# Gate projections of a decoder layer: seven-product pairs fed by one transfer each, fewer of them, their sums spread out

## The chip, the cores and the metric

The kernel runs on one core of a Trainium2 chip. The metric is the device time of one execution in microseconds. The times shown are medians of several executions of the same program.

## The reference

One layer of a hybrid decoder for 16 learned and 256 given positions of width 2048, in float32. Only the part that the change touches is told closely.

```python
h = h + 0.5 * swiglu(rms_norm(h), ...)                  # first feed-forward half step
z = rms_norm(h) @ w_in                                  # one projection, 11 parts
q, k, v, qi, ki, wi, xc, gate_b, gate_c, ga, gc = split(z)
y_attn = sparse_attention(q, k, v, qi, ki, wi) @ w_attn_branch
y_conv = (gate_b * causal_conv3(gate_c * xc)) @ w_conv_branch
merged = sigmoid(ga) * y_attn + sigmoid(gc) * y_conv    # the gate stage computes this line
h = h + merged @ w_out
h = h + 0.5 * swiglu(rms_norm(h), ...)                  # second feed-forward half step
```

`ga` and `gc` are each 256 positions by 2048 columns, with 2048 inputs: two matrix products of 256 x 2048 by 2048 x 2048.

## The kernel before

**Splitting of weights.** Every float32 weight block arrives by DMA in a tile `raw` (SP issues the transfers), is rounded by ScalarE into `whi` (line 227), and VectorE writes the rest `raw - whi` into `wlo` (line 228). Activations are split in the same way. Each product is three matmuls: high by high, high by low, low by high (`mac3`, lines 613 to 615, for products in which the tokens are the stationary operand and 512 weight columns move).

**The stream.** The class `Stream` holds the list of all weight transfers (`loads`) and of the parts of them that are split in one go (`subs`, at most 1024 columns). `next` hands out one weight block after another. When a part is used up it runs what is due, then splits the part that lies three ahead, then runs the `later` list. The split tiles have four buffers, so the split of a part can begin only when TensorE has finished the part four before it. Each engine works through its instructions in the order in which they are written, so whatever is written ahead of a `wlo` on VectorE delays it.

**The ring.** `raw` has 12 slots of 512 columns (256 KB each). A transfer is issued as soon as the slots it wants have been split (`load`); it then waits for the splits of their former owner.

**Gate stage.** The 2048 output columns are done in four blocks `c` of 512 (`gates(c)`), for `ga` and `gc` together. The 2048 inputs form eight pairs of 256. One pair is a product of a 2 by 2 arrangement: two token tiles and two input tiles on one side, two input tiles and two outputs (`ga`, `gc`) on the other. Kind `C` does it with the plain eight products of four weight blocks, accumulated in the PSUM banks `q2`, `q3`, `q4`, `q8`. The other kind does it with seven products, as Strassen and Winograd do: the weight side needs sums of the blocks, the token side needs sums of the token tiles, which are made once per pair (`sums_of_tokens`, tiles `made`) and used in all four column blocks, and seven banks collect the products. At the end of a block `recombine` (lines 696 to 701) turns banks `q1`, `q5`, `q6`, `q7` into the four results, one step after another, and `after_end` (line 1193) adds what the plain pairs collected.

After the eight pairs come the branch products of the block: `y_attn` and `y_conv` by 512 columns, 32 products into the banks `pbr`. `merge` (lines 1218, 1220) multiplies gates and branches at the start of the next block. Ahead of the last half pair the merged block before is turned by TensorE (`pt`, line 666) and split into `ms` (lines 438, 439).

**Kind Q, the seven-product pair of before.** It takes two loads of four blocks `[a21, a22, a11, a12]` (the order in memory), and a second time the last three of them in two more loads: 7 blocks of 256 KB. `sum_ahead` (line 212) makes the four sums in place in the first four blocks, one directly after the other, when the part before them is about to be split. The plain blocks for the other products are the second copy. Parts of the pair: 2, 2, 2 and 1 blocks.

Block 0 takes the kinds `CCCQQQCC`, the later blocks `CQQCQQCC`; `SEVEN` lists the pairs with sums of tokens, (3, 5, 7, 1), made while block 0 runs.

Around the stage nothing is touched: the convolution stage before it, the output projection `po` (line 417) after it and the second feed-forward, which has seven-product pairs of another kind (`P`, whose sums are made long before and stored).

Of the kernel before, what the change touches and what calls it, by code (L numbers as in the profile page):

```python
# [9 lines left out]
F32 = mybir.dt.float32  # L10
# [5 lines left out]
P = 128  # L16
D = 2048
# [34 lines left out]
WIDE = 512  # L52
NG = FF // WIDE
PAIRS = KD // 2
# [3 lines left out]
PLAN = [step for gs in PARTS for step in [("up", g) for g in gs] + [("down", gs)]]  # L58


SEVEN = (3, 5, 7, 1)
SUMS = ((1, 1, 0), (0, 0, 2), (2, 2, 1), (3, 3, 2))
SEVEN2 = (3, 5, 7, 1, 6)
LATE = (8, 4)
# [5 lines left out]


def pairs_gate(c):
    return list(zip("CCCQQQCC", [0, 2, 4, 3, 5, 7, 6, 1]) if c == 0 else zip("CQQCQQCC", [0, 3, 5, 2, 7, 1, 4, 6]))


def pairs_down(gs, half):
# [21 lines left out]
class Stream:  # L98
# [7 lines left out]
    def __init__(self, nc, raw, split_pool):  # L106
        self.nc = nc
        self.ring = [(raw, i) for i in range(2 * SLOTS)]
        self.owner, self.pos = {}, 0
        self.split_pools, self.ahead, self.n_tiles = [split_pool], AHEAD, 0  # L110
        self.loads, self.subs = [], []
        self.raw, self.ready, self.summed = {}, {}, set()
        self.n_loaded = self.n_split = self.at = 0
        self.blocks, self.waiting, self.steps = [], [], []
        self.first = []
        self.ahead_of, self.prep = [], []
# [13 lines left out]
    def add_pair(self, kind, four, ahead):  # L130

        if kind == "C":
            self.add(four.pop(0), 4, WIDE, False)
            return
        if kind == "P":
            src, made = ahead.pop(0)
            self.ahead_of.append((src, made))
            self.add(made, 4, WIDE, False)
            self.add(src[:, WIDE:], 3, WIDE, False)
            return  # L140
        src = ahead.pop(0)
        g = len(self.subs)
        self.add(src, 4, WIDE, False)
        self.add(src[:, WIDE:], 3, WIDE, False)
        self.subs[g] = (self.subs[g][0], "sums") + self.subs[g][2:]

    def widen(self, raw, split_pool):

# [54 lines left out]

    def sum_ahead(self):

        for g, kind, _, _, _ in self.subs[self.n_split : self.n_split + 2]:
            if kind == "sums" and g not in self.summed:
                self.load(g + 2)
                self.summed.add(g)
                x = [self.raw[g + j // 2][:, j % 2 * WIDE : (j % 2 + 1) * WIDE] for j in range(4)]  # L210
                for out, a, b in SUMS:
                    self.nc.vector.tensor_add(x[out], x[a], x[b])

    def split(self, upto):
        nc = self.nc
        while self.n_split < min(upto, len(self.subs)):
            self.sum_ahead()
            g, kind, c, kk, width = self.subs[self.n_split]
            self.load(len(self.loads))
            n = kk * width  # L220
            raw = self.raw[g][:, c : c + n]
            pool = self.split_pools[self.n_tiles % len(self.split_pools)]
            self.n_tiles += 1
            hi = pool.tile([P, SUB], F32R, name="whi")
            lo = pool.tile([P, SUB], F32R, name="wlo")
            to = [x[:, :n] for x in (hi, lo)]
            nc.scalar.activation(to[0], raw, AF.Copy)  # L227
            nc.vector.tensor_sub(to[1], raw, to[0].bitcast(F32))  # L228
            self.ready[self.n_split] = [
                (hi[:, i * width : (i + 1) * width], lo[:, i * width : (i + 1) * width]) for i in range(kk)  # L230
            ]
            self.n_split += 1
            self.load(len(self.loads))
# [48 lines left out]
def tile_decoder_layer(  # L282
# [13 lines left out]
    wq: bass.AP,  # L296
    wcv: bass.AP,
    wg: bass.AP,
    wgq: bass.AP,
    wb: bass.AP,  # L300
    wo: bass.AP,
    w2: bass.AP,
# [14 lines left out]
    st = Stream(nc, raw_pool.tile([P, SLOTS * SUB], F32, name="raw"), split_pool)  # L317
# [18 lines left out]
    chunks(wq, 0, 8, 512)  # L336
    units2 = len(st.subs)
    chunks(wcv, 0, 3 * KC)
    wg_c, wg_q, w2_c, w2_p = ([w[i] for i in range(w.shape[0])] for w in (wg, wgq, w2, w2p))
    scratch = ctx.enter_context(tc.tile_pool(name="scratch", bufs=1, space=bass.MemoryType.DRAM))  # L340
    w2_p = [(w, scratch.tile([P, RAW], F32, name=f"sums{i}")) for i, w in enumerate(w2_p)]
    for c in range(D // WIDE):
        for kind, _ in pairs_gate(c):
            st.add_pair(kind, wg_c, wg_q)
        for i in range(KC // 2):
            st.add(wb[c * KC // 2 + i], 4, WIDE, False)
    for a, b in ((0, 12), (12, KD)):
# [8 lines left out]
    h = hp.tile([P, KD, T], F32, name="h")  # L356
# [5 lines left out]
    small = const.tile([P, SMALL], F32, name="small")  # L362
    ident = const.tile([P, P], F32, name="ident")
# [314 lines left out]
    def group(todo, hook, after_seven, after_end, spread=(1, 2, 3, 4)):  # L678

        kinds = [k for k, _, _ in todo]  # L680
        nc_ = kinds.count("C")
        ns = len(kinds) - nc_
        last = max(n for n, k in enumerate(kinds) if k != "C")
        q = {}

        def of(tag):
            if tag not in q:
                q[tag] = [bank(tag, tag), 0, {"q2": ns + 2 * nc_, "q3": ns + 2 * nc_, "q4": ns + 2 * nc_, "q8": 2 * nc_}.get(tag, ns)]
            return q[tag]

        buf = {}

        def recombine():
            a, v, x, e = (small_tile(n) for n in "avxe")
            buf.update(q2=a, q3=v, q4=x, q8=e)
            nc.scalar.activation(a, q["q1"][0], AF.Copy)
            steps = [
                lambda: nc.vector.tensor_sub(v, q["q6"][0], a),
                lambda: nc.vector.tensor_add(x, q["q7"][0], v),
                lambda: nc.vector.tensor_sub(v, q["q5"][0], v),  # L700
                lambda: nc.vector.scalar_tensor_tensor(e, q["q5"][0], -1.0, x, op0=ALU.mult, op1=ALU.add),
            ]
            soon = spread and not spread[0]
            if soon:
                steps[0]()
            for i, fn in list(enumerate(steps))[bool(soon) :]:
                st.later(fn, spread[i] if spread else 1)
            if after_seven:
                for i, tag in enumerate(buf):
                    st.later(lambda tag=tag: after_seven(tag, buf[tag]), 5 + i // 2 if spread else 2)  # L710

        for n, (kind, four, ts) in enumerate(todo):
            b11, b12, b21, b22 = four()
            if kind != "C":
                t1, t3, t2, t4 = (both(ts()[:, :, f * P : (f + 1) * P]) for f in range(4))
                todo7 = [("q7", t3), ("q5", t1), ("q6", t2), ("q3", b22), ("q4", t4), ("q1", b11), ("q2", b21)]
                for tag, t in todo7:
                    mac3(of(tag), t, st.next())
                if n == last:
                    st.early(recombine)  # L720
            else:
                plain_half(b11, b12, b21, b22, of("q2"), of("q3"))
                if n == len(todo) - 1:
                    st.early(lambda: after_end(q, buf, ("q2", "q3")))
                hook(n)
                plain_half(b11, b12, b21, b22, of("q4"), of("q8"), not spread and n == len(todo) - 1)
        st.early(lambda: after_end(q, buf, ("q4", "q8")))

    with ExitStack() as mix:
# [434 lines left out]
        gp = mix.enter_context(tc.tile_pool(name="gates", bufs=1, reuse_waits="tile"))  # L1164
        room.append(gp)

        act1 = act[:, :, :, LATER + META : LATER + T]
        made1 = {i: gp.tile([P, 2, 4 * P], F32R, name=f"made{i}") for i in SEVEN}
        for at, (i, to) in zip((0, 3, 7, 16), made1.items()):
            sums_of_tokens(i, gains[1], to, at)  # L1170

        ms, merged = {}, []
# [233 lines left out]


_INS = [
    "h", "small", "rope", "cbias", "ident", "wgu1", "wd1", "wk", "wkw", "wv", "wqi", "wq", "wcv", "wg", "wgq", "wb",
    "wo", "w2", "w2p",  # L1410
]

# [27 lines left out]
def _quads(kind, w0, w1, i, j0, j1):  # L1440

    rows = [w[2 * i * P : (2 * i + 2) * P, j * WIDE : (j + 1) * WIDE].reshape(2, P, WIDE) for w, j in ((w0, j0), (w1, j1))]
    (a11, a12), (a21, a22) = rows
    return np.concatenate(
        {"C": [a12, a11, a22, a21], "P": [a21, a22, a11, a12], "Q": [a21, a22, a11, a12]}[kind], 1
    )


def _by_kind(chunks, kinds):
    return [np.stack([x for k, x in chunks if k == kind]) for kind in kinds]  # L1450


def _gates(ga, gc):
    return _by_kind([(k, _quads(k, ga, gc, i, c, c)) for c in range(D // WIDE) for k, i in pairs_gate(c)], "CQ")


def _second(wg, wu, wd):
# [34 lines left out]
def _layout(x, meta_tokens, ffn1_norm_g, ffn1_w_gate, ffn1_w_up, ffn1_w_down, mix_norm_g, w_in, q_norm_g,  # L1492
# [21 lines left out]
    w = w_in[0]  # L1514
# [4 lines left out]
    a["wkw"] = _tiles(np.concatenate([ki, wi], 1), NKW)[0]  # L1519
    a["wqi"], a["wq"] = _chunks(_tiles(qi, 512)), _chunks(_tiles(q, 512))  # L1520
    a["wcv"] = np.stack([_tiles(xc, P), _tiles(gc_, P), _tiles(gb, P)], 1).reshape(3 * KC, P, KD * P)
    a["wg"], a["wgq"] = _gates(ga, gcv)
    wb = np.stack([w_attn_branch[0], w_conv_branch[0]]).reshape(2, KC, P, D // WIDE, WIDE).transpose(3, 1, 2, 0, 4)
    a["wb"] = np.ascontiguousarray(
        wb.reshape(D // WIDE, KC // 2, 2, P, 2 * WIDE).transpose(0, 1, 3, 2, 4).reshape(-1, P, RAW)
# [23 lines left out]
```

## Time and profile before

| what | value |
|---|---|
| median of three executions | 2140.4 us (2139.38 to 2141.89) |
| the profiled execution | 2142.07 us, its span 2140.3 us |
| granted TensorE clock, mean | 0.997 |
| busy TensorE, weight loads, VectorE, ScalarE | 2113.4, 1904.6, 1676.7, 1132.9 us |
| DMA | 617.24 MB, 288 GB/s on average |
| gate stage | 1087.1 to 1362.9 us |

PE is TensorE's matmuls, PEld its weight loads (they overlap), DVE VectorE, ACT ScalarE, POOL GpSimd, SP the engine that issues the weight transfers. A line of a timeline gives start, duration, engine, source line, operation, `out<-in` with tile names, shape and count; in brackets stands the idle time ahead of it and what ended it. A matmul row lasts longer than its share of the engine, since matmuls are pipelined: the distance from one start to the next tells the rate. A line of the list of waits gives the waiting engine with its instruction, what it waited for, the total in us, how often, and the longest.

### The profile page before, as it was taken

Reading aid. Unit: us, or ns where it says so; the run is one execution under the profiler, and the core shown is the slowest. Engines: PE = TensorE matmul, PEld = TensorE weight load, DVE = VectorE, ACT = ScalarE, POOL = GpSimd, SP = SyncE. Lnnn points to the kernel's source line nnn. Section 1 sums busy time; section 2 is a strip of 40 time slices with the busy share of each in tenths; the row PEclk is TensorE's granted clock in tenths of the full one; section 3 lists DMA queues with packets and bytes.
Section 4 is the critical chain, followed back from the end, with each engine's and each line's share of the span. In section 5 each row is a group of like instructions: output and inputs, shape, how many; then the busy total and the mean of one; then the engine's idle time right before and its main releaser. Section 6 shows DMA issues by size and latency. Waiting matters only on the chain.

```text
span 2140.3 us, 33445 instructions
## 1 busy us (share of the span) xinstructions
PE 2113.4 (99%) x12961; PEld 1904.6 (89%) x12961; DVE 1676.7 (78%) x2214; ACT 1132.9 (53%) x1469; POOL 114.8 (5%) x190
## 2 busy tenths in 40 slices
PE   8999999999999999999999999999999999999999
PEld 8999999999999999889987877888888888888887
DVE  7777766677777767887787878587888888988887
ACT  5444433344444445465455555476766667666664
POOL 2000000000000110000000000010000000000000
PEclk9999999999999999999999999999999999999999
DMA  7899999999999967845676677467787888788875
GB/s 282 307 350 360 361 350 371 355 360 364 352 369 354 358 232 256 348 172 198 239 235 223 228 252 229 163 225 245 274 314 282 287 319 303 292 274 301 310 268 177
DMA packets 128895, 617.24 MB, mean 288 GB/s; under 512 B 14336, under 2 KB 14464, under 8 KB 86624
## 3 DMA queue, kind: packets, MB, share of 16 engines
q1 hardware_dynamic: 107712, 463.52, 60.6%
q0 software_dynamic: 20880, 151.42, 18.8%
q8 instruction: 101, 1.65, 0.3%
q14 instruction: 58, 0.48, 0.1%
q10 hardware_dynamic: 144, 0.17, 0.0%
HBM read 537.46 MB, written 77.59 MB: 287 GB/s over the span
## 4 chain that ended last, share of the span: by engine, by line
PE 92%; DVE 4%; DMA 2%; ACT 1%; issue 1%; POOL 0%; SPq 0%; ACTq 0%; DVEq 0%
PE q L614 12%; PE q L615 12%; PE q L613 12%; PE pd L402 4%; PE pd L403 4%; PE pd L404 4%; PE pg L404 4%; PE pu L404 4%; PE pg L402 4%; PE pu L402 4%; PE pg L403 4%; PE pu L403 4%; PE po L417 3%; DVE wlo L228 2%; PE po L419 1%; PE pbr L613 1%
## 5 line engine op out<-in xcount | busy, mean ns | idle before, releaser
L227 ACT ACTIVATE whi<-raw 128x1024 fp32r<-128x1024 f32 (+2 forms) x927 | 926.9, 1011 | 903.1 <-PE q L615 264.3
L228 DVE TENSOR_TENSOR wlo<-raw,whi 128x1024 fp32r<-128x1024 f32 (+2 forms) x927 | 1060.5, 1164 | 396.7 <-ACT whi L227 385.5
L614 PE MATMUL q<-wlo,act 128*128 128x512 f32 x713 | 279.5, 392 | 11.3 <-DVE wlo L228 11.3
L613 PE MATMUL q<-whi,act 128*128 128x512 f32 x713 | 280.0, 393 | 0.0
L615 PE MATMUL q<-whi,act 128*128 128x512 f32 x713 | 279.2, 392 | 0.0
L167 DVE TENSOR_TENSOR prep<-prep 128x512 f32<-128x512 f32 x288 | 196.9, 684 | 15.7 <-DMA prep<-in_w2p_dram 15.5
L402 PE MATMUL pd<-mid,whi 128*128 128x272 f32 x704 | 201.7, 286 | 0.0
L403 PE MATMUL pd<-mid,whi 128*128 128x272 f32 x704 | 201.7, 286 | 0.0
L404 PE MATMUL pd<-mid,wlo 128*128 128x272 f32 x704 | 201.7, 286 | 0.0
L402 PE MATMUL pg<-act,whi 128*128 128x272 f32 x672 | 192.7, 287 | 0.0
L404 PE MATMUL pg<-act,wlo 128*128 128x272 f32 x672 | 192.5, 287 | 0.0
L403 PE MATMUL pg<-act,whi 128*128 128x272 f32 x672 | 192.5, 287 | 0.0
L402 PE MATMUL pu<-act,whi 128*128 128x272 f32 x672 | 192.5, 286 | 0.0
L403 PE MATMUL pu<-act,whi 128*128 128x272 f32 x672 | 192.5, 286 | 0.0
L404 PE MATMUL pu<-act,wlo 128*128 128x272 f32 x672 | 192.5, 286 | 0.0
L614 PEld LDWEIGHTS q<-wlo,act 128*128 128x128 f32 x713 | 134.6, 189 | 40.5 <-DVE wlo L228 13.0
L615 PEld LDWEIGHTS q<-whi,act 128*128 128x128 f32 x713 | 134.7, 189 | 28.2
L613 PEld LDWEIGHTS q<-whi,act 128*128 128x128 f32 x713 | 134.6, 189 | 27.5
L402 PEld LDWEIGHTS pd<-mid,whi 128*128 128x128 f32 x704 | 132.6, 188 | 0.0
L403 PEld LDWEIGHTS pd<-mid,whi 128*128 128x128 f32 x704 | 132.6, 188 | 0.0
L404 PEld LDWEIGHTS pd<-mid,wlo 128*128 128x128 f32 x704 | 132.6, 188 | 0.0
L403 PEld LDWEIGHTS pg<-act,whi 128*128 128x128 f32 x672 | 126.6, 188 | 0.0
(273 smaller groups left out, 3802.5 us busy)
## 6 DMA issues: line engine op xcount, KB each, us to landing
raw<-in_wgu_dram SPq DMA_DIRECT2D x87, 1024.0 KB, 6.5
prep<-in_w2p_dram POOLq DMA_DIRECT2D x72, 1024.0 KB, 9.1
sums<-prep POOLq DMA_DIRECT2D x72, 1024.0 KB, 5.7
raw<-sums SPq DMA_DIRECT2D x144, 512.0 KB, 5.7
raw<-in_w_dram SPq DMA_DIRECT2D x120, 512.0 KB, 6.4
raw<-in_wd_dram SPq DMA_DIRECT2D x44, 1024.0 KB, 8.1
raw<-in_w2p_dram SPq DMA_DIRECT2D x72, 512.0 KB, 5.7
raw<-in_wcv_dram SPq DMA_DIRECT2D x24, 1024.0 KB, 4.8
```

The lines of the kernel that those rows point to most:

```text
L167: nc.vector.tensor_add(x[out], x[a], x[b])
L227: nc.scalar.activation(to[0], raw, AF.Copy)
L228: nc.vector.tensor_sub(to[1], raw, to[0].bitcast(F32))
L402: nc.tensor.matmul(ps, whi, xhi, start=first, stop=False)
L403: nc.tensor.matmul(ps, whi, xlo, start=False, stop=False)
L404: nc.tensor.matmul(ps, wlo, xhi, start=False, stop=last)
L417: nc.tensor.matmul(ps.rearrange("p (a t) -> p a t", a=2), whi, x(i), start=i == 0, stop=False)
L419: nc.tensor.matmul(ps[:, :SEQ], wlo, x(i)[:, 0, :], start=False, stop=i == total - 1)
L613: nc.tensor.matmul(ps, xhi, whi, start=n == 0, stop=False)
L614: nc.tensor.matmul(ps, xhi, wlo, start=False, stop=False)
L615: nc.tensor.matmul(ps, xlo, whi, start=False, stop=n == total - 1)
```

## The change

A new kind `S` takes the place of `Q` in the gate stage.

- An S pair is loaded once, four blocks `[a21, a11, a22, a12]` in two loads.
- Three of its sums go into a new tile `extra` of 3 x 512 columns, one is made in place. Parts of the pair: `extra` 0 and 1; the two blocks of the first load, the first of them now a sum; the two blocks of the second load; `extra` 2.
- The four sums are made in three goes (two, one, one), each just ahead of the split of the part before the one that needs them. A part whose sums cannot be made yet, since `extra` does not exist before the stage, is not split.
- The seven products come in another order, to follow the parts.
- Block 0 takes `CCCSCSCC` with its pairs in their natural order, the later blocks `CSSCSCCC`. So there are 2 + 3 x 3 = 11 seven-product pairs instead of 3 + 3 x 4 = 15. Pair 1 becomes plain everywhere, its sums of tokens are not made, and those of pair 7 are made later.

```diff
-SEVEN = (3, 5, 7, 1)
+SEVEN = (3, 5, 7)
...
-    return list(zip("CCCQQQCC", [0, 2, 4, 3, 5, 7, 6, 1]) if c == 0 else zip("CQQCQQCC", [0, 3, 5, 2, 7, 1, 4, 6]))
+    return list(zip("CCCSCSCC", range(PAIRS)) if c == 0 else zip("CSSCSCCC", [0, 3, 5, 1, 7, 2, 4, 6]))
...
-        src = ahead.pop(0)
-        g = len(self.subs)
-        self.add(src, 4, WIDE, False)
-        self.add(src[:, WIDE:], 3, WIDE, False)
-        self.subs[g] = (self.subs[g][0], "sums") + self.subs[g][2:]
+        g, n = len(self.loads), len(self.subs)
+        self.add(ahead.pop(0), 4, WIDE, False)
+        self.subs[n:] = [(g, "sums", 0, 2, WIDE), (g, "raw", 0, 2, WIDE), (g + 1, "raw", 0, 2, WIDE), (g + 1, "sums", 2 * WIDE, 1, WIDE)]
+
+        def add(*abc):
+
+            def block(i):
+                x = self.extra if i < 3 else self.raw[g + (i - 3) // 2]
+                i = i if i < 3 else (i - 3) % 2
+                return x[:, i * WIDE : (i + 1) * WIDE]
+
+            def fn():
+                self.load(g + 2)
+                for to, a, b in abc:
+                    self.nc.vector.tensor_add(block(to), block(a), block(b))
+
+            return fn
+
+        self.sums.update({n: add((0, 3, 4), (1, 3, 5)), n + 1: add((3, 1, 4)), n + 2: add((2, 3, 6))})
...
-        for g, kind, _, _, _ in self.subs[self.n_split : self.n_split + 2]:
-            if kind == "sums" and g not in self.summed:
-                self.load(g + 2)
-                self.summed.add(g)
-                x = [self.raw[g + j // 2][:, j % 2 * WIDE : (j % 2 + 1) * WIDE] for j in range(4)]
-                for out, a, b in SUMS:
-                    self.nc.vector.tensor_add(x[out], x[a], x[b])
+        for n in (self.n_split, self.n_split + 1):
+            if n in self.sums and self.extra is not None:
+                self.sums.pop(n)()
...
             self.sum_ahead()
+            if self.n_split in self.sums:
+                return
...
-            raw = self.raw[g][:, c : c + n]
+            raw = (self.extra if kind == "sums" else self.raw[g])[:, c : c + n]
...
                 todo7 = [("q7", t3), ("q5", t1), ("q6", t2), ("q3", b22), ("q4", t4), ("q1", b11), ("q2", b21)]
+                if kind == "S":
+                    todo7 = [todo7[i] for i in (0, 1, 2, 5, 4, 6, 3)]
...
+        st.extra = gp.tile([P, 3 * WIDE], F32, name="extra")
         act1 = act[:, :, :, LATER + META : LATER + T]
         made1 = {i: gp.tile([P, 2, 4 * P], F32R, name=f"made{i}") for i in SEVEN}
-        for at, (i, to) in zip((0, 3, 7, 16), made1.items()):
+        for at, (i, to) in zip((0, 3, 16), made1.items()):
```

More of the change, by code (lines that the diff above doesn't have):

```diff
@@ L111, in __init__ @@
         self.loads, self.subs = [], []
-        self.raw, self.ready, self.summed = {}, {}, set()
+        self.raw, self.ready, self.sums, self.extra = {}, {}, {}, None
         self.n_loaded = self.n_split = self.at = 0
@@ L298, in tile_decoder_layer @@
     wg: bass.AP,
-    wgq: bass.AP,
+    wgs: bass.AP,
     wb: bass.AP,
@@ L338, in tile_decoder_layer @@
     chunks(wcv, 0, 3 * KC)
-    wg_c, wg_q, w2_c, w2_p = ([w[i] for i in range(w.shape[0])] for w in (wg, wgq, w2, w2p))
+    wg_c, wg_s, w2_c, w2_p = ([w[i] for i in range(w.shape[0])] for w in (wg, wgs, w2, w2p))
     scratch = ctx.enter_context(tc.tile_pool(name="scratch", bufs=1, space=bass.MemoryType.DRAM))
@@ L343, in tile_decoder_layer @@
         for kind, _ in pairs_gate(c):
-            st.add_pair(kind, wg_c, wg_q)
+            st.add_pair(kind, wg_c, wg_s)
         for i in range(KC // 2):
@@ L1408 @@
 _INS = [
-    "h", "small", "rope", "cbias", "ident", "wgu1", "wd1", "wk", "wkw", "wv", "wqi", "wq", "wcv", "wg", "wgq", "wb",
+    "h", "small", "rope", "cbias", "ident", "wgu1", "wd1", "wk", "wkw", "wv", "wqi", "wq", "wcv", "wg", "wgs", "wb",
     "wo", "w2", "w2p",
@@ L1444, in _quads @@
     return np.concatenate(
-        {"C": [a12, a11, a22, a21], "P": [a21, a22, a11, a12], "Q": [a21, a22, a11, a12]}[kind], 1
+        {"C": [a12, a11, a22, a21], "P": [a21, a22, a11, a12], "S": [a21, a11, a22, a12]}[kind], 1
     )
@@ L1453, in _gates @@
 def _gates(ga, gc):
-    return _by_kind([(k, _quads(k, ga, gc, i, c, c)) for c in range(D // WIDE) for k, i in pairs_gate(c)], "CQ")
+    return _by_kind([(k, _quads(k, ga, gc, i, c, c)) for c in range(D // WIDE) for k, i in pairs_gate(c)], "CS")
 def _second(wg, wu, wd):
@@ L1521, in _layout @@
     a["wcv"] = np.stack([_tiles(xc, P), _tiles(gc_, P), _tiles(gb, P)], 1).reshape(3 * KC, P, KD * P)
-    a["wg"], a["wgq"] = _gates(ga, gcv)
+    a["wg"], a["wgs"] = _gates(ga, gcv)
     wb = np.stack([w_attn_branch[0], w_conv_branch[0]]).reshape(2, KC, P, D // WIDE, WIDE).transpose(3, 1, 2, 0, 4)
```

## The prediction

> **What bounds the kernel now.** I read the page first (busy times, then the chain of work that ended last), then the waits cut to the stretch that the diff touches, then a table of that stretch by stage, then the timelines of TensorE and VectorE around each stall.
>
> ```profile
> span 2140.3 us, 33445 instructions
> ...
> PE 2113.4 (99%) x12961; PEld 1904.6 (89%) x12961; DVE 1676.7 (78%) x2214; ACT 1132.9 (53%) x1469; POOL 114.8 (5%) x190
> ```
>
> TensorE is never idle for long: 26.9 us of 2140.3. So time can only be won where it waits or runs slowly, and every matmul added is paid in full. The waits between 1080 and 1365 us, which hold the gate stage:
>
> ```profile
> PE q L614 <- DVE wlo L228: 11.7, 6, 3.4
> ...
> DVE raw L212 <- DMA raw<-in_wgq_dram: 9.4, 6, 2.6
> ...
> PE pbr L613 <- DVE ms L439: 1.4, 2, 1.2
> ```
>
> The first row is the same (11.7 us) in the list for the whole kernel: all of it lies here. Next the gate stage, cut at the first matmul of each block's pairs and of its branch products (columns: window, its length, then busy time with instruction count of PE, PEld, DVE, ACT, POOL, then the granted clock, DMA share, GB/s):
>
> ```profile
> 1087.10:1134.00 46.90, 44.16 (x185) 35.22 (x184) 41.86 (x59) 27.83 (x37) 0.73 (x1) 0.96 0.73 245
> 1134.00:1155.76 21.76, 21.76 (x97) 18.02 (x96) 14.69 (x16) 12.12 (x13) 0.00 (x0) 1.00 0.58 176
> 1155.76:1202.65 46.89, 43.62 (x189) 35.63 (x188) 41.30 (x49) 24.88 (x27) 0.00 (x0) 0.96 0.78 261
> 1202.65:1224.41 21.76, 21.76 (x97) 18.02 (x96) 14.54 (x17) 10.95 (x12) 0.00 (x0) 1.00 0.56 163
> 1224.41:1271.44 47.03, 43.65 (x190) 35.62 (x188) 41.29 (x49) 24.77 (x27) 0.00 (x0) 0.96 0.76 257
> 1271.44:1293.20 21.76, 21.76 (x98) 18.02 (x96) 14.55 (x17) 10.95 (x12) 0.00 (x0) 1.00 0.55 170
> 1293.20:1339.19 45.99, 43.65 (x189) 35.63 (x188) 39.92 (x48) 24.08 (x26) 0.00 (x0) 0.96 0.78 251
> 1339.19:1362.92 23.73, 22.28 (x98) 17.86 (x96) 12.76 (x16) 11.44 (x15) 0.00 (x0) 1.00 0.56 195
> ```
>
> A branch stage has 16 weight blocks x 2 token tiles x 3 matmuls = 96, and runs without a gap: 21.76 / 96 = 0.227 us a matmul, 0.68 us a product of three. That is the ruler. Block 0 has 3 Q and 5 C pairs, 3x7 + 5x8 = 61 products; the later ones 4x7 + 4x8 = 60, and 0.79 us of transposes, which stand in the middle of the last pair:
>
> ```profile
> 1199.03 1.03 PE L666 MATMUL pt<-ident,vm 128*128 128x128 f32 x8
> 1199.82 0.47 PE L613 MATMUL q<-whi,act 128*128 128x512 f32 x1
> ```
>
> So the four pair stages should last 41.5, 41.6, 41.6, 41.6 us, and lose 5.4, 5.3, 5.4 and 4.4; the last branch stage loses 23.73 - 21.76 = 2.0. Together **22.5 us**, twice the 11.7 of the wait list. The other half is in the matmuls behind a stall:
>
> ```profile
> 1115.71 0.50 PE L614 MATMUL q<-wlo,act 128*128 128x512 f32 x1 [2.32 <-DVE wlo L228]
> ...
> 1177.11 0.50 PE L614 MATMUL q<-wlo,act 128*128 128x512 f32 x1 [3.27 <-DVE wlo L228]
> ...
> 1178.69 0.63 PE L614 MATMUL q<-wlo,act 128*128 128x512 f32 x1
> 1179.11 0.63 PE L615 MATMUL q<-whi,act 128*128 128x512 f32 x1
> ...
> 1245.88 0.50 PE L614 MATMUL q<-wlo,act 128*128 128x512 f32 x1 [3.38 <-DVE wlo L228]
> ...
> 1313.62 0.50 PE L614 MATMUL q<-wlo,act 128*128 128x512 f32 x1 [2.34 <-DVE wlo L228]
> ```
>
> After the wait the matmuls follow 0.43 us apart, not 0.23, for about eight of them; the window's granted clock is 0.96 against 1.00 in the branch stages. Of block 1's 5.3 us, 3.4 are the gap and 1.9 the slow clock. The other three long waits have their slow stretch behind them too.
>
> Why the wait? VectorE around block 1, then the link that the chain of work shows between its last `wlo` and the late sum:
>
> ```profile
> 1155.53 0.69 DVE L1218 TENSOR_TENSOR va<-pbr,va 128x512 f32<-128x512 f32 x1
> ...
> 1159.12 2.35 DVE L228 TENSOR_TENSOR wlo<-raw,whi 128x1024 fp32r<-128x1024 f32 x2
> 1161.39 2.86 DVE L212 TENSOR_TENSOR raw<-raw 128x512 f32<-128x512 f32 x4
> 1164.17 5.83 DVE L228 TENSOR_TENSOR wlo<-raw,whi 128x512 fp32r<-128x512 f32 x6
> 1172.45 0.69 DVE L212 TENSOR_TENSOR raw<-raw 128x512 f32<-128x512 f32 x1 [2.45 <-DMA raw<-in_wgq_dram]
> ```
> ```profile
> 1167.15 6.54 DMA raw<-in_wgq_dram
> ```
>
> The third Q pair's sums stand in VectorE's queue ahead of a `wlo` that TensorE needs sooner, and wait there for a load that could start only at 1167.15, when a `wlo` of the second pair freed its slots. A Q takes 7 of the ring's 12 slots, so the ring reaches 1.7 pairs ahead. Block 0 has no such DMA wait: there three Q in a row with the sums of tokens simply overfill VectorE:
>
> ```profile
> 1103.81 2.87 DVE L212 TENSOR_TENSOR raw<-raw 128x512 f32<-128x512 f32 x4
> ```
>
> **The change, part by part.**
>
> *Matmuls.* Block 0 goes from 3 seven-product pairs to 2, the others from 4 to 3: one product more each, 4 x 3 x 0.227 = **+2.7 us**, on the path with nothing to cover it.
>
> *Loads.* A Q brings 1.75 MB in four transfers, an S 1 MB in two, like a C. 15 Q + 17 C make 43.25 MB, 11 S + 21 C 32 MB; 30 fewer issues on SP. Every pair now takes 4 slots, so the ring reaches 3 pairs. When is the load for block 1's third S due? Count from 1155.76 as 0. It takes the slots of the first S's second load, free when that pair's last `wlo` is done, about 8.0 (below). The landing times of these loads:
>
> ```profile
> DMA to landing us min/median/max: 2.8/4.4/6.9
> ```
>
> So it is there at 12.5, or 15 at worst; its first sum comes up on VectorE at 14.4 and TensorE does not need what stands behind it until 17.9. The DMA wait goes; what is late next is VectorE itself.
>
> *VectorE per pair.* The number of sums stays four per pair. The rows price them: four in a burst 1161.39 to 1164.17, 0.70 each, where each waits for the one ahead of it; independent ones of this size start 0.60 apart (1155.53 to 1159.12, six). A full `wlo` is 2.27 / 2 = 1.13, a half one 0.60. An S so costs 2.4 to 2.8 + 3 x 1.13 + 0.6 = 6.4 to 6.8 us against 4.76 us of its matmuls; a C 2.3 against 5.44. I take 0.60 for a sum, since the new order puts a `wlo` between dependent ones, and keep 0.70 for the bound.
>
> *Order.* The sums now come as two, one and one, each ahead of another `wlo`. Block 1 is C S S C S C C C. By the rows above, VectorE merges the branches from -0.23 until 3.36, with the first S's first `wlo` already behind it. Then: third sum of S1 3.96, `wlo` 5.10, 6.23, two sums of S2 7.43, S1's half `wlo` 8.03, sum 8.63, `wlo` of S2's first part 9.77 (TensorE wants it at 10.21 + 0.23 = 10.44), sum 10.37, `wlo` of the second 11.50 plus 0.09 to be seen (wanted 11.80), third 12.64 (13.16), half 13.24 (14.5), C 14.38 (15.2), two sums of S4 15.58, `wlo` 16.7 (17.9). The tightest point has 0.2 us. With sums at 0.70, five of them ahead of it, it is 0.3 late. ACT is not in the way: `whi` of that part can start when the sum is done at 8.63 and takes 1.06. I book 0.3 us a block, from 0 to 0.8.
>
> *Block 0.* C C C S C S C C: the S stand apart, and S plus C is 6.4 + 2.3 = 8.7 on VectorE against 10.2 on TensorE. The sums of tokens for pair 1 fall away, those for pair 7 move to the late place. I book 0.2.
>
> *Last branch stage.* The wait there is for `ms`, which stands behind two steps of `recombine` (700, 701):
>
> ```profile
> 1336.25 0.68 DVE L700 TENSOR_TENSOR vv<-q,vv 128x512 f32<-128x512 f32 x1
> ...
> 1339.78 0.42 DVE L439 TENSOR_TENSOR ms<-pt,ms 128x256 fp32r<-128x256 f32 x1
> ```
>
> In the later blocks the last seven-product pair is now the fifth, not the sixth, so these two steps (1.2 us) come one pair earlier. Of 2.0 us, 0.5 stay (0 to 2.0).
>
> *Tile `extra`.* The next pair's two sums overwrite it three parts after their last reader; no wait. It and one `made` tile fewer shift later tiles of the pool; their former users are a stage old. Nothing, with the first C pair (8 x 0.68 = 5.4 us) as cover: the first sum comes up only behind it; without that cover the first sum would wait for the last user of the old pool.
>
> *A rule beside the rows.* The slow stretch follows waits of 2.3 to 3.4 us, four times of four, and is absent in the branch stages. The Trainium skill (TensorE: Matmul & The Clock Gate, Part 1) has the clock halve after at least one idle window of about 3.4 us, free-running. Taken by the letter, these waits would be too short, the slow stretch would have another cause and stay; see the third rival.
>
> **Sum.** -22.5 (all lost time) + 2.7 (matmuls) + 0.3 x 3 + 0.2 + 0.5 (what stays lost) = **-18.2 us**, -0.85%. The profiled execution took 2142.07 us (span 2140.3, 1.8 around it), 1.7 above the median of 2140.4; against the median that makes **2122.2**. With nothing left lost: 2140.4 - 19.8 = 2120.6.
>
> **Rivals.**
>
> 1. *VectorE stays late at two S in a row, and the clock drops behind it.* A stall of 0.5 us with the slow stretch of 1.9 in three blocks: 7.2 instead of 0.9, so -11.9: 2128.5. For it: the margin of 0.2 us after 11.7 us of unbroken VectorE work. Against: the sums got cheaper, and the slow stretch followed no wait under 2.3 us (the 1.2 us wait at `pbr` had none).
> 2. *The DMA wait stays in the three later blocks.* Only block 0 is cured: -5.4 + 2.7: 2137.7, within 0.2%. It decides if the third S's load lands after about 16, 8 us after its slots are free; the slowest landing so far is 6.9.
> 3. *The slow stretches have another cause.* About 2.1 + 3 x 1.9 = 7.8 us stay lost: 2130. Against it stands their place, right behind each wait and nowhere else in the stage. The rule above gives this result.
> 4. *Slower: VectorE and ACT alternate instead of overlapping within an S*, since each part's `whi` now waits for a sum that stands behind the part before. Then an S takes (1.4 + 1.06 + 1.22) + (0.7 + 1.06 + 1.22) + 2.3 + 2.0 = 11 us against 4.76; two in a row run 12.5 behind, a lead of some 5 covers part, with the slow clock 9 us a block instead of the 5.0 on average now: 3 x 4 + 2.7 - 5.4 = +9: 2150. It decides from about 2.5 us more per S. Against: each sum stands ahead of a `wlo` that belongs to an earlier part, so ACT works under it.
>
> **How the numbers follow.** Main case 0.75, rivals 0.10, 0.05, 0.04 and 0.04, the rest unnamed and on both sides. Two executions differ by some 0.1% here (2139.38 to 2141.89), so 0.2%, 4.3 us, is what can be told from no change. Faster: main, first and third rival, 0.90; same: the second, 0.05; slower: the fourth and unnamed, 0.05. The range takes the main case with its bounds (nothing lost 2120.6, 1.5 less for the runs' spread; bounds of what stays lost 2125) and rivals 1 and 3: 2119 to 2132.
>
> **What would show it.** Pair stages of 42.2 us in block 0 (62 products) and 42.3 to 43 in the later ones (61), granted clock 1.00 in all; no VectorE wait for gate loads; the TensorE wait on `wlo` under 2 us in sum; the last branch stage near 22.3. Wrong if a wait of over 2 us sits at the second S of a block, or if the loads of the third S still end one.

## The result and the profile after

| | before | after |
|---|---|---|
| median of 20 executions | 2140.35 us (2137.74 to 2142.36) | 2122.95 us (2122.60 to 2123.43, and one of 2143.54) |
| ratio after / before | | 0.9923, 95% interval 0.9912 to 0.9934 |
| gate stage in the profile | 275.8 us | 256.9 us |
| granted clock, mean | 0.997 | 1.000 |

The change took 17.4 us off, 0.8%. The one execution of 2143.54 us was the one that was profiled: its matmuls of 272 columns, in stages that the change does not touch, last 290 ns each instead of the 286 of every other profile here, and why is not known. So the profile shown is that of another execution of the same kernel (2123.11 us, span 2121.3). Its gate stage lasts 256.88 us, in the odd execution 256.88 too.

The gate stage by the same cuts (window, length, busy time of PE, PEld, DVE, ACT, POOL with counts, granted clock, DMA share, GB/s):

```profile
1087.27:1129.45 42.18, 42.18 (x188) 34.93 (x187) 37.62 (x53) 25.38 (x33) 1.32 (x2) 1.00 0.74 241
1129.45:1151.21 21.76, 21.76 (x97) 18.02 (x96) 14.08 (x16) 12.11 (x13) 0.00 (x0) 1.00 0.63 192
1151.21:1193.71 42.50, 42.50 (x192) 35.11 (x191) 37.86 (x45) 23.09 (x25) 0.00 (x0) 1.00 0.63 201
1193.71:1215.47 21.76, 21.76 (x97) 18.02 (x96) 13.04 (x15) 10.94 (x12) 0.00 (x0) 1.00 0.64 191
1215.47:1257.95 42.48, 42.48 (x193) 35.10 (x191) 37.85 (x45) 23.07 (x25) 0.00 (x0) 1.00 0.62 200
1257.95:1279.71 21.76, 21.76 (x98) 18.02 (x96) 13.05 (x15) 10.94 (x12) 0.00 (x0) 1.00 0.65 191
1279.71:1322.17 42.46, 42.46 (x192) 35.11 (x191) 37.38 (x45) 23.03 (x26) 0.00 (x0) 1.00 0.62 198
1322.17:1344.15 21.98, 21.98 (x98) 17.95 (x96) 11.46 (x14) 10.78 (x13) 0.00 (x0) 1.00 0.55 181
```

The stage starts where it did (1087.3, before 1087.1). Its pair stages fell from about 47 to 42.2 and 42.5 us although each has three matmuls more; TensorE's busy time equals the length of every window, and the clock is full throughout. The complete list of TensorE's waits in this execution holds nothing of the gate stage any more:

```profile
PE start L414 <- ACT whi L239: 6.3, 1, 6.3
PE pcg L416 <- DVE wlo L240: 0.9, 2, 0.6
PE start L416 <- DVE wlo L240: 0.8, 1, 0.8
PE start L414 <- ACT act L464: 0.7, 1, 0.7
PE start L415 <- DVE act L465: 0.6, 1, 0.6
PE pqt L911 <- DVE zz L814: 0.3, 1, 0.3
```

VectorE's queue in block 1 (the block starts at 1151.21; line 240 is `wlo`, 155 the sums):

```profile
1153.97 0.69 DVE L1235 TENSOR_TENSOR vm<-vv,ve 128x512 f32<-128x512 f32 x1
1154.57 0.69 DVE L155 TENSOR_TENSOR extra<-raw 128x512 f32<-128x512 f32 x1
1155.17 2.36 DVE L240 TENSOR_TENSOR wlo<-raw,whi 128x1024 fp32r<-128x1024 f32 x2
1157.44 1.29 DVE L155 TENSOR_TENSOR extra<-raw 128x512 f32<-128x512 f32 x2
1158.64 0.69 DVE L240 TENSOR_TENSOR wlo<-extra,whi 128x512 fp32r<-128x512 f32 x1
1159.25 0.69 DVE L155 TENSOR_TENSOR raw<-extra,raw 128x512 f32<-128x512 f32 x1
1159.95 1.23 DVE L240 TENSOR_TENSOR wlo<-extra,whi 128x1024 fp32r<-128x1024 f32 x1
1161.09 0.69 DVE L155 TENSOR_TENSOR extra<-raw 128x512 f32<-128x512 f32 x1
1161.69 2.35 DVE L240 TENSOR_TENSOR wlo<-raw,whi 128x1024 fp32r<-128x1024 f32 x2
```

No row has an idle time in brackets: from the merge on VectorE works without a break worth listing and without a DMA wait, and it is just fast enough. TensorE at the tightest point:

```profile
1162.78 0.39 PE L625 MATMUL q<-whi,made 128*128 128x512 f32 x1
1163.00 0.47 PE L626 MATMUL q<-wlo,made 128*128 128x512 f32 x1
1163.31 0.39 PE L627 MATMUL q<-whi,made 128*128 128x512 f32 x1
```

The matmul with the second part's `wlo` of the second S, 11.79 us after the block's start, is the only one of the block off the 0.23 us beat, by 0.08 us, apart from the transposes and the matmul behind them.

### The profile page after: what moved, and what is told of

Read it like the earlier page. It is cut to its first block, busy times and chain, and to the rows that moved or that the text cites. A ratio compares the mean times of both kernels' runs of the same rounds, so it can differ in the third digit from the quotient of the medians.

```text
span 2141.7 us, 33310 instructions
## 1 busy us (share of the span) xinstructions
PE 2128.3 (99%) x12973; PEld 1923.8 (90%) x12973; DVE 1657.2 (77%) x2186; ACT 1125.3 (53%) x1458; POOL 114.5 (5%) x190
## 4 chain that ended last, share of the span: by engine, by line
PE 97%; DMA 1%; DVE 1%; ACT 1%; POOL 0%; issue 0%; SPq 0%
PE q L625 13%; PE q L626 13%; PE q L627 13%; PE pd L414 4%; PE pd L416 4%; PE pd L415 4%; PE pu L415 4%; PE pg L415 4%; PE pu L414 4%; PE pg L414 4%; PE pu L416 4%; PE pg L416 4%; PE po L429 3%; PE po L431 1%; PE pbr L625 1%; PE pbr L627 1%
## 5 line engine op out<-in xcount | busy, mean ns | idle before, releaser
L240 DVE TENSOR_TENSOR wlo<-raw,whi 128x1024 fp32r<-128x1024 f32 (+2 forms) x897 | 1035.1, 1172 | 432.3 <-ACT whi L239 420.4
L239 ACT ACTIVATE whi<-raw 128x1024 fp32r<-128x1024 f32 (+2 forms) x897 | 902.4, 1017 | 889.2 <-PE q L627 254.2
L625 PE MATMUL q<-whi,act 128*128 128x512 f32 x733 | 286.5, 391 | 0.0
L627 PE MATMUL q<-whi,act 128*128 128x512 f32 x733 | 285.4, 389 | 0.0
L626 PE MATMUL q<-wlo,act 128*128 128x512 f32 x733 | 285.4, 389 | 0.0
L415 PE MATMUL pd<-mid,whi 128*128 128x272 f32 x704 | 203.9, 290 | 0.0
L414 PE MATMUL pd<-mid,whi 128*128 128x272 f32 x704 | 203.9, 290 | 0.0
L627 PEld LDWEIGHTS q<-whi,act 128*128 128x128 f32 x733 | 137.6, 188 | 28.6
L625 PEld LDWEIGHTS q<-whi,act 128*128 128x128 f32 x733 | 137.7, 188 | 28.0
```

The source lines that it names most:

```text
L414: nc.tensor.matmul(ps, whi, xhi, start=first, stop=False)
L415: nc.tensor.matmul(ps, whi, xlo, start=False, stop=False)
L625: nc.tensor.matmul(ps, xhi, whi, start=n == 0, stop=False)
L626: nc.tensor.matmul(ps, xhi, wlo, start=False, stop=False)
L627: nc.tensor.matmul(ps, xlo, whi, start=False, stop=n == total - 1)
```

## The experiments

Theory: in blocks 1 to 3 TensorE waited because the ring reached only 1.7 pairs ahead, so the third Q's loads came late and its sums held up a `wlo` in VectorE's queue; in block 0 because three Q in a row were too much for VectorE. Rivals: what helped is that there are fewer seven-product pairs; or that the sums come spread out; or that the DMA moves fewer bytes.

**The changed kernel again** (no edit).

> The changed kernel once more, for an undisturbed profile. Theory (the gain lies in the gate stage alone, TensorE waits and the slow clock behind them): the stage starts at about 1087 us, as in the profile of before, and lasts 256.9 us against 275.8; the time is 2123. If instead the matmuls of 272 columns in the first feed-forward are really slower in the changed kernel (0.1265 us apart in its first profile, 0.1238 before), the stage starts near 1107 again.

2123.35 us (2123.11 to 2123.63). The stage starts at 1087.27, and the matmuls of the first feed-forward are those of before:

```profile
L414 PE MATMUL pd<-mid,whi 128*128 128x272 f32 x704 | 201.7, 286 | 0.0
```

So the whole gain between the two profiles lies in the gate stage: 275.82 - 256.88 = 18.9 us.

**Fewer pairs alone.**

```diff
 (kernel before)
-SEVEN = (3, 5, 7, 1)
+SEVEN = (3, 5, 7)
-    zip("CCCQQQCC", [0, 2, 4, 3, 5, 7, 6, 1]) if c == 0 else zip("CQQCQQCC", [0, 3, 5, 2, 7, 1, 4, 6])
+    zip("CCCQCQCC", range(PAIRS)) if c == 0 else zip("CQQCQCCC", [0, 3, 5, 1, 7, 2, 4, 6])
```

> Before, with kind Q kept (four loads, 7 slots, the four sums in one burst), only the placing of the change: CCCQCQCC and CQQCQCCC, pair 1 plain. Theory (the later blocks wait for a load that is late because a Q takes 7 of 12 slots; block 0 is VectorE work alone): the wait at the third Q stays in blocks 1 to 3 (5.3, 5.4, 4.4 us lost), block 0 is cured (-5.2), the last branch stage too (-1.5), 12 matmuls more (+2.7): 2140.4 - 4.0 = 2136. Rival (fewer seven-product pairs, so less VectorE work, are what helps): nearly as the changed kernel, 2123 to 2126.

2136.23 us (ratio 0.9979, 0.9969 to 0.9988). The four pair stages and the list of waits in the gate stage:

```profile
1087.28:1129.80 42.52, 42.49 (x189) 34.85 (x188) 36.23 (x49) 25.29 (x32) 0.74 (x1) 1.00 0.75 248
...
1151.56:1196.13 44.57, 42.70 (x193) 35.06 (x191) 37.88 (x44) 23.19 (x25) 0.00 (x0) 1.00 0.77 258
...
1217.89:1267.24 49.35, 45.43 (x192) 37.06 (x191) 37.87 (x44) 23.18 (x25) 0.00 (x0) 0.93 0.71 233
...
1289.00:1335.32 46.32, 44.31 (x192) 36.20 (x191) 37.42 (x44) 23.13 (x26) 0.00 (x0) 0.96 0.74 246
```
```profile
PE q L614 <- DVE wlo L228: 7.8, 3, 3.9
DVE raw L212 <- DMA raw<-in_wgq_dram: 7.2, 6, 2.3
```

VectorE's work in a later block is the same as after the change (37.9 us in both), block 0 is cured, and yet the three later blocks still have one long wait each, with VectorE waiting for the gate loads. They lose 2.3, 7.0 and 4.0 us (before: 5.3, 5.4 and 4.4). Fewer pairs in other places give 4 of the 17 us.

**Kind S, as many pairs as before.**

```diff
 (changed kernel; the sums of tokens for pair 1 are made again, as before)
-SEVEN = (3, 5, 7)
+SEVEN = (3, 5, 7, 1)
-    zip("CCCSCSCC", range(PAIRS)) if c == 0 else zip("CSSCSCCC", [0, 3, 5, 1, 7, 2, 4, 6])
+    zip("CCCSSSCC", [0, 2, 4, 3, 5, 7, 6, 1]) if c == 0 else zip("CSSCSSCC", [0, 3, 5, 2, 7, 1, 4, 6])
```

> The changed kernel with kind S in the old places: CCCSSSCC and CSSCSSCC, 15 seven-product pairs again, pair 1 among them. Theory (the load was the cause in the later blocks): by the order of VectorE's queue with 0.60 us a sum the second pair of S S just fits too, 0 to 0.3 us lost a block; block 0 with three S in a row runs late by 1 to 4 us, slow clock included; 12 matmuls fewer (-2.7): 2121 to 2125, and the stages of blocks 1 to 3 last 41.6 to 42.2 us. Rival (VectorE is over its limit with four, the fewer pairs are the gain): blocks 1 to 3 lose 4 to 5 us each again, 2135 to 2138.

2125.58 us (ratio 0.9931, 0.9915 to 0.9948), half a microsecond above the theory's range. Blocks 0 and 1:

```profile
1087.63:1133.39 45.76, 44.10 (x186) 35.26 (x184) 41.29 (x59) 27.84 (x37) 0.74 (x1) 0.96 0.63 199
...
1155.15:1197.19 42.04, 42.04 (x189) 34.45 (x188) 40.79 (x50) 24.55 (x27) 0.00 (x0) 1.00 0.61 202
```

The later blocks run four S in 42.0 us each, without a wait, 4 to 5 us faster than with four Q and 0.4 us faster than with three S. So three of eight is not what cured them; it is kind S itself, by its transfers or by the order of its sums, and the next experiments tell these apart. Block 0 shows the other cause alone: three S in a row lose 45.8 - 41.5 = 4.3 us, with two waits for `wlo` of 0.8 us each and no DMA wait. Which of three things cures it in the changed kernel (two pairs instead of three, a plain pair between them, one set of sums of tokens fewer) is not separated. The last branch stage, which waits for `ms` again, lost 1.0.

**All four sums at once.**

```diff
 (changed kernel; the third sum of alternate pairs goes to a fourth 512 columns of extra)
-        self.sums.update({n: add((0, 3, 4), (1, 3, 5)), n + 1: add((3, 1, 4)), n + 2: add((2, 3, 6))})
+        self.sums.update({n: add((0, 3, 4), (1, 3, 5), (3, 1, 4), (2, 3, 6))})
```

> The changed kernel, but all four sums of an S in one go ahead of the part before it, as Q had them (the third sum of alternate pairs goes to a fourth 512 columns of the extra tile, so that it is not overwritten early). Theory (loads, not the order of the sums): the second S of two in a row is about 0.4 to 0.8 us late in blocks 1 to 3, without a slow stretch behind: 2123 to 2125.5. Rival (spreading the sums is what removed the wait): 4 to 5 us lost a block, 2135 to 2138.

2123.79 us; the later blocks last 42.6 us each. With three S a block, spreading the sums is worth 0.1 to 0.2 us a block.

**The ring's slots back, then the bytes alone.** The first gives each S two more transfers into the ring, the second three more into spare columns through GpSimd's queue; nobody reads them.

```diff
 (changed kernel, slots and bytes)
+        self.loads += [(src[:, : 2 * WIDE], 2 * WIDE), (src[:, 3 * WIDE :], WIDE)]
```

> The changed kernel, but each S brings two more transfers (512 and 256 KB) into the ring that nobody reads: 7 slots and 1.75 MB a pair, as Q had; sums, order and pairs as changed. Theory (the ring's reach was the cause in the later blocks): the third S's loads come too late again, its sums stand in VectorE's queue and wait for a DMA, TensorE loses 0.5 to 5 us a block, slow clock included: 2125 to 2138, the DMA wait of VectorE is back in the list. Rival (fewer pairs or the order of the sums): no change, 2123.

```diff
 (changed kernel, bytes alone; extra is 5 * WIDE wide; j over blocks 0, 1 and 3 of each pair)
+                    self.nc.gpsimd.dma_start(self.extra[:, (3 + j % 2) * WIDE : (4 + j % 2) * WIDE], src[:, j * WIDE : (j + 1) * WIDE])
```

> The changed kernel, but each S reads 0.75 MB more over another queue (GpSimd's) into spare columns that nobody reads: the bytes of Q, but no slots of the ring. Theory (reach, not bandwidth): 2123 to 2124, no DMA wait. Rival (the DMA's bandwidth in the S S stretch, 3.5 MB in 10 us, is the cause): as with the slots, 2125 to 2138.

With the slots: 2133.82 us (ratio 0.9975, 0.9965 to 0.9984), 10.5 above the changed kernel. Blocks 1 to 3, and the waits:

```profile
1151.40:1196.43 45.03, 43.08 (x192) 34.94 (x191) 37.92 (x45) 23.19 (x25) 0.00 (x0) 1.00 0.73 246
1218.19:1265.51 47.32, 44.66 (x192) 36.09 (x191) 38.10 (x45) 23.19 (x25) 0.00 (x0) 0.96 0.70 234
1287.27:1332.10 44.83, 43.10 (x193) 34.94 (x191) 37.37 (x45) 23.14 (x26) 0.00 (x0) 1.00 0.73 247
```
```profile
DVE extra L157 <- DMA raw<-in_wgs_dram: 6.4, 4, 2.0
PE q L628 <- DVE wlo L242: 6.3, 6, 2.4
```

When block 1's third S gets its second load, first in the changed kernel (SP issues it), then with the slots (the transfer, and the sum that waits for it):

```profile
1157.56 0.33 SPq L215 DMA_DIRECT2D raw<-in_wgs_dram  x1
```
```profile
1164.25 5.65 DMA raw<-in_wgs_dram
...
1169.93 0.69 DVE L157 TENSOR_TENSOR extra<-raw 128x512 f32<-128x512 f32 x1 [1.66 <-DMA raw<-in_wgs_dram]
```

That is 6.4 and 12.9 us after the block's start. Both times the issue follows a `wlo` that frees the slots (in the second case one that ends at 1164.24), so the load is late because it waits for slots. In flight it took 4.6 and 5.7 us: of the delay, 6.5 us are the wait for slots and 1.1 the longer flight.

With the bytes alone: 2123.30 us. GpSimd's queue ran ahead, so all the extra bytes fell into blocks 0 and 1; block 1 is the test:

```profile
1150.99:1193.48 42.49, 42.49 (x193) 35.11 (x192) 37.85 (x46) 23.08 (x25) 6.19 (x12) 1.00 0.83 277
```

277 GB/s is more than the 261 of block 1 before, and nothing is late. The extra bytes did slow the ring's own loads of S (median to landing 4.5 us against 4.0 in the changed kernel), and still none of them was late. Same kernel, same sums, same pairs: 7 slots a pair bring the DMA wait back, the same bytes outside the ring do not. The reach of the ring was the cause in blocks 1 to 3. A larger ring was not tried.

**Waits of a chosen length.** Idle additions on VectorE ahead of the tightest `wlo`, another number in each block:

```diff
 (changed kernel; more = 2, 4, 6 or 3, 5, 8 for the second S of blocks 1, 2, 3, else 0; extra is 4 * WIDE wide)
             def fn():
                 self.load(g + 2)
+                for _ in range(more if abc[0][0] == 2 else 0):
+                    self.nc.vector.tensor_add(self.extra[:, 3 * WIDE :], block(3), block(6))
```

> The changed kernel with idle additions on VectorE (0.60 us each, results unused) ahead of the second part's wlo of the second S: 2, 4 and 6 of them in blocks 1, 2 and 3. TensorE there has no slack (0.06 us late already), so it should wait about 1.3, 2.5 and 3.7 us. Theory (the slow clock follows a wait of 2.3 us or more, about 8 matmuls at 0.43 us, 1.9 us lost): none behind the first, one each behind the other two; stages 43.7, 46.8, 48.0; 2123.2 + 7.5 + 3.8 = 2134. Rival (it takes an idle time of about 3.4 us, by the Trainium skill, TensorE: Matmul & The Clock Gate, Part 1, an estimate from that page): behind the third only.

> The same with 3, 5 and 8 idle additions: waits of about 1.9, 3.1 and 4.9 us. Theory: the slow clock certainly behind the last two, the first is near the edge; 2123.2 + 9.9 + 3.8 to 5.7 = 2137 to 2139. Rival (an idle time of about 3.4 us is needed): behind the last only, 2135.

2135.8 and 2137.28 us, from a single execution each; the first is 1.8 above what was expected, the second as expected. The waits were 1.13, 2.58 and 4.03 us, then 1.85, 3.30 and 5.48: each idle addition made them 0.73 us longer, not 0.60, since all write the same columns and each waits for the one ahead. First run, blocks 1 and 2, then the second run's block 1:

```profile
1164.16 0.50 PE L630 MATMUL q<-wlo,made 128*128 128x512 f32 x1 [1.13 <-DVE wlo L244]
...
1231.18 0.50 PE L630 MATMUL q<-wlo,made 128*128 128x512 f32 x1 [2.58 <-DVE wlo L244]
...
1232.52 0.63 PE L629 MATMUL q<-whi,made 128*128 128x512 f32 x1
1232.94 0.63 PE L630 MATMUL q<-wlo,made 128*128 128x512 f32 x1
```
```profile
1164.72 0.50 PE L630 MATMUL q<-wlo,made 128*128 128x512 f32 x1 [1.85 <-DVE wlo L244]
1165.06 0.39 PE L631 MATMUL q<-whi,made 128*128 128x512 f32 x1
```

Behind 2.58 us the matmuls come 0.42 us apart, behind 1.13 and 1.85 they do not. All single waits of the profiled executions in this stage that were over 1 us, in order of length, with the number of matmuls behind them that are followed by the next one after 0.40 to 0.43 us:

| wait, us | 1.13 | 1.18 | 1.30 | 1.37 | 1.85 | 1.87 | 2.01 | 2.32 | 2.34 | 2.40 | 2.58 | 3.27 | 3.30 | 3.38 | 3.92 | 4.03 | 5.48 |
|---|---|---|---|---|---|---|---|---|---|---|---|---|---|---|---|---|---|
| slow matmuls | 0 | 0 | 0 | 0 | 0 | 0 | 8 | 8 | 7 | 7 | 7 | 7 | 6 | 7 | 12 | 13 | 7 |

In these 17 waits the edge lies between 1.87 and 2.01 us, not at 3.4. It is not a matter of one wait's length alone. In the kernel with three S in a row, waits of 0.75 and 0.76 us less than 2 us apart, with a hitch of 0.3 just ahead, were followed by 8 slow matmuls; in the next kernel below, waits of 0.46 and 0.77 us in the same place were followed by none:

```profile
1115.37 0.50 PE L626 MATMUL q<-wlo,made 128*128 128x512 f32 x1 [0.77 <-DVE wlo L240]
```

So short waits seem to add up, which two cases suggest but do not show. Nor do the slow matmuls always begin at once: in 6 of the 11 cases, as in the first run above (1231.18 and 1232.52), 1.1 to 1.6 us of matmuls came between at the full rate or nearly so. The Trainium skill (TensorE: Matmul & The Clock Gate, Part 1) asks for about 3.4 us of idle time in a free-running window; the runs agree that the slow stretch follows idle time and costs half the rate, and disagree on the length that it takes.

**More seven-product pairs.**

```diff
 (changed kernel, with a fourth made tile for pair 1)
-    zip("CCCSCSCC", range(PAIRS)) if c == 0 else zip("CSSCSCCC", [0, 3, 5, 1, 7, 2, 4, 6])
+    zip("CCSCSSCC", [0, 2, 3, 4, 5, 7, 6, 1]) if c == 0 else zip("CSSCSSCC" if c < 3 else "CSSCSCCC", [0, 3, 5, 2, 7, 1, 4, 6])
```

> Kind S with as many seven-product pairs as VectorE can feed: block 0 CCSCSSCC (three, the first apart), blocks 1 and 2 CSSCSSCC (four, as they ran in 42.0 us), block 3 CSSCSCCC (three, so that recombine is over before the last half pair). 14 seven-product pairs instead of 11: 9 matmuls fewer. Theory (VectorE's queue keeps up wherever at most two S stand together behind a C): block 0 lasts 41.5 to 42, blocks 1 and 2 42.05 each, block 3 42.5, the last branch stage 22.0; 2123.2 - 1.5 = 2121.7, at best 0.07% faster than the changed kernel. Rival (the first S of block 0 comes too early for its sums of tokens, and VectorE is behind from there on): block 0 lasts 43 to 45, 2123 to 2125.

> The changed kernel on the same chip and in the same rounds, to compare with: 2123.2, from 2122.6 to 2123.6.

2123.52 us (2123.44 to 2124.31) against 2123.22 (2122.76 to 2123.42) of the changed kernel in the same rounds: the rival's numbers held. Blocks 1 to 3 ran as expected (42.1, 42.1, 42.5), block 0 took 44.0 with two waits for `wlo`. The rival's reason held only in part: the waits stand at the last S, not at the first, and on VectorE the sums of tokens for pair 7 stand between the two S of the later group:

```profile
1108.87 0.42 DVE L656 TENSOR_TENSOR vm<-vm 128x256 f32<-128x256 f32 x1
...
1110.99 0.68 DVE L451 TENSOR_TENSOR made<-vm,made 128x512 fp32r<-128x512 f32 x1
```

Whether moving them alone would cure block 0 was not tried. In the last kernel block 0 has the changed kernel's form again, and only blocks 1 and 2 keep four S:

```diff
 (changed kernel, with a fourth made tile for pair 1)
-    ... else zip("CSSCSCCC", [0, 3, 5, 1, 7, 2, 4, 6])
+    ... else zip("CSSCSSCC" if c < 3 else "CSSCSCCC", [0, 3, 5, 2, 7, 1, 4, 6])
-        for at, (i, to) in zip((0, 3, 16), made1.items()):
+        for at, (i, to) in zip((0, 3, 13, 16), made1.items()):
```

> Block 0 and block 3 as in the changed kernel, blocks 1 and 2 with four S (CSSCSSCC): 13 seven-product pairs instead of 11, 6 matmuls fewer. Theory: block 0 42.2 us, blocks 1 and 2 42.05 instead of 42.47 each: 0.85 us faster than the changed kernel, 2122.4. Rival (a fourth made tile and its sums of tokens in block 0, two at the end, delay block 0 or its branch products): no gain, 2123.2 or more.

> The changed kernel in the same rounds: 2123.2, from 2122.6 to 2123.6.

2122.43 us (2122.28 to 2122.63) against 2122.89 (2122.77 to 2123.29): 0.5 us faster, half of what was expected, the fastest kernel of the study. Its blocks 1 and 2, which take 42.49 and 42.48 us in the changed kernel's profile of these rounds:

```profile
1151.18:1193.28 42.10, 42.10 (x190) 34.46 (x188) 40.84 (x50) 24.55 (x27) 0.00 (x0) 1.00 0.60 202
1215.04:1257.35 42.31, 42.25 (x189) 34.41 (x188) 41.07 (x51) 24.56 (x27) 0.00 (x0) 1.00 0.59 200
```

## Why the prediction was right

It gave 2122.2 us, 2119 to 2132; measured 2122.95.

- *22.5 us of lost time, half wait and half slow clock.* The sum is right: all of it but 0.8 us is gone, the slow stretches with the waits. The halves are not: in the rows of before, the waits for `wlo` take 11.7, those for `ms` 1.4, and 29 matmuls at 0.43 us cost 5.8; the remaining 3.6 lie in single distances next to the waits and at either end of the slow stretches. This did no harm, since all of it hung on the waits. The third rival (another cause of the slow stretches) is out. The rule of the Trainium skill (TensorE: Matmul & The Clock Gate, Part 1), read by the letter, would have left the slow stretches in place, and the runs go against it.
- *2.7 us for 12 matmuls.* Right: block 0 lasts 42.18, and 62 x 0.68 is 42.2.
- *The DMA wait goes since the ring reaches 3 pairs.* Right, and shown from both sides: Q with the new placing keeps the wait, S with Q's slots gets it back. The load in question had more room than predicted: issued at 6.4 us instead of 8.0, there at 10.9 instead of 12.5, with its first sum at 14.5 (14.4). Its slots are free before the pair's last `wlo`, which reads `extra`. One line was misread: the load that started at 1167.15 ended only at 1173.69, and held up the second sum, at 1173.78; the 2.45 us at 1172.45 were ended by the load ahead of it, issued at 1166.02. The mechanism is the same. The prediction reckoned with landing times up to 6.9 us; the median and the longest are shorter now:

```profile
DMA to landing us min/median/max: 3.5/4.0/5.2
```

- *VectorE's order in block 1.* Predicted (after 1151.21) 3.96, 6.23, 7.43, 8.03, 9.77, 10.37, 11.50; the rows above have 3.96, 6.23, 7.43, 8.04, 9.88, 10.48, and with the two `wlo` from 1161.69 11.6. The one difference is the `wlo` at 1159.95, which starts 0.70 us behind the sum ahead of it instead of 0.60. It waited for ScalarE, whose `whi` of that part could begin only when the part's second sum was done, and ended at 1159.92:

```profile
1158.85 1.06 ACT L239 ACTIVATE whi<-extra 128x1024 fp32r<-128x1024 f32 x1 [1.32 <-DVE extra L155]
```

  The prediction had cleared ScalarE for another part only. The tightest point was the named one, late by 0.08 us where 0.3 was booked.
- *What stays lost.* Booked 1.6 (0.2 in block 0, 0.3 in each later one, 0.5 in the last branch stage); measured about 0, 0.2 each (42.5 against 61 x 0.68 + 0.79 = 42.3) and 0.2. The gate stage so gained 18.9 instead of 18.2.
- *From the profile to the median.* This step failed, by 1.5 us, and hid the one above: the gain was taken off the median whole, as if the profiled execution's 1.7 us over the median lay elsewhere. They lay in the stage itself: outside it the two profiled executions agree (start at 1087.1 and 1087.3, from its end to the span's end 777.4 and 777.2 us). So the waits' lengths seem to differ from one execution to the next, which fits the spread of 4.6 us before and of 0.8 after, the odd execution aside; of before only one execution was profiled. Taken off the profiled execution's own time, 2142.07 - 18.9 = 2123.1. That the forecast of 2122.2 came within 0.8 us is in part luck: a gain booked 0.7 too small and a start 1.7 too low pull opposite ways.
- *Rivals.* The second (the DMA wait stays) is what the kernel with Q and three pairs did: 2136.2. The fourth (ScalarE and VectorE alternate) showed only in the one `wlo` above, by 0.1 us; the 2.5 us per S that it would take did not occur.

## What to carry to other kernels

Count a load ring's reach in units of what is consumed, not in bytes: a pair that takes 7 of 12 slots leaves less than two pairs of foresight, and then a cheap VectorE instruction that waits for a load holds up everything behind it in its queue. Price a TensorE wait with the clock: in this stage a single one of 2 us or more cost 1.2 to 2.6 us on top, in slow matmuls, and one of up to 1.9 none. And where a wait varies from run to run, take the gain off the execution that was profiled, not off the median.

## What the runs showed of the hardware that was not expected

The slow clock followed every single wait of 2.01 us and more and none between 1 and 1.87 us, in 17 waits of five kernels, always at 0.43 us a matmul of 512 columns instead of 0.227 and for 6 to 13 matmuls, beginning at the wait's end or up to 1.6 us after it. How long it lasted did not grow steadily with the wait (7 behind 5.48 us, 13 behind 4.03). Independent additions of 128x512 on VectorE start 0.60 us apart, and 0.73 apart where each waits for the one before.
